# A decoder block on one core: longer runs for the table loads of the second half, fewer split buffers, four banks for the quad sums

## The chip, the core and the metric

The kernel runs on one core of a Trainium2 chip. The core has five engines that work through their own instruction streams and meet only at semaphores: TensorE (PE, matrix products, which loads its weights beside them), VectorE (DVE), ScalarE (ACT), GpSimd (POOL) and SyncE (SP, which here only issues DMAs). All DMAs of the core run on the same 16 DMA engines, whichever engine issued them. The metric is the time of one execution on the device in microseconds; the figure for a kernel is the median of several runs.

## The reference

One layer of a decoder for 256 tokens of width 2048, in float32, with two sub-layers and a last RMSNorm. The first mixes tokens (a recurrent branch and a state-space branch behind one projection). The second is the one that this change touches, a retrieval over 128 x 128 = 16384 single-neuron experts:

```python
h2 = rms_norm(x, norm2_g) * (1.0 + scale2) + shift2
# 8 heads; each picks its 16 best experts out of 16384 by product keys; gate = softmax of the 16 scores
u = jnp.take(u_tab, e, axis=0)                       # the chosen rows of the table u, 2048 wide
act = jax.nn.gelu(jnp.einsum("td,thkd->thk", xt, u))
v = jnp.take(v_tab, e, axis=0)                       # the same rows of the table v
out = jnp.einsum("thk,thkd->td", g * act, v)
return x + gate2 * out                               # then the last RMSNorm
```

So each token needs 128 rows of the table u for dot products, and 128 rows of the table v for a weighted sum.

## The kernel before

The experts are ordered in 128 columns of 128. Their first 100 columns are handled in a mixed way, the last 28 densely.

**The u quads** (`u_quad`, from line 1488). For the first 100 columns all dot products are computed: 25 quads of four columns, each 256 tokens x 512 experts. A quad takes eight items of the table u; an item is 128 x 1024 floats, 512 KB. An item holds, for the four columns of its quad, 256 of the 2048 features (two blocks of 128). A float32 product is made of three products of parts that TensorE takes at full speed, so a product of a and b is high(a) x high(b), low(a) x high(b), high(a) x low(b): lines 1496 to 1498, twelve matmuls for each item, each 512 wide. The sums of a quad lie in two of the banks 0, 1, 2, taken in turn, one for each half of the tokens. ACT copies them out (line 1502) to the tile X2, and a store writes them to memory.

**The stream of items** (lines 130 to 160). All weights and tables go through one list of items in the order of use. `issue_dma` loads the next item into one of four buffers `raw` (NRAW). `issue_split` makes an item's high part on ACT (line 149, L149), and one item later `issue_lo` makes its low part on DVE (line 158, L158), into one of four tiles `hl` (NHL), and then issues the load of the item that takes the buffer. `take` gives the next `hl` to the matmuls. A tile `hl` is free for a split when TensorE has finished the item four places before. Loads of u items of the quads are issued by SP; from the u slots on, SP and ACT issue them in turn.

**The sparse quads.** Of the first 100 columns each token uses only some 100 experts. When the lists of the chosen experts are ready, POOL gathers the dot products by address (words, line 1572, into `lsm`), ACT and DVE make the weights from them (`w_make`, the tiles Wz), and POOL gathers the rows of v, 128 rows of 8 KB at a time, into one of seven row buffers (tk, vx, vq; line 1559). `v_quad` (line 1607) multiplies four gathers with their weights: 16 matmuls, which the trace shows as 32, into the banks 4 to 7. There are 54 such quads in three groups: 12 for the first half of the tokens from the first 44 columns, then 27 for the second half of the tokens, then 15 for the first half again. `tick`, called once for each item of a u quad and of a slot, decides while the program is written where the next sparse quad stands in TensorE's order (`due`), and feeds POOL's queue (`w_feed`, `v_feed`). Nothing is decided on the chip.

**The dense rest.** 28 u slots (`u_slot`, two items each) and 56 v slots (`v_slot`, one item each, line 1714) handle the last 28 columns without gathers: 4 KB runs, half a row of the table for each partition.

**The end of a group.** The sums of the first group are copied by ACT to the tile S0 (line 1613). Those of the second group are scaled by gate2 and added to x on DVE directly from the banks (`merge`, lines 1741 and 1743, four times). `rows_load` loads the rows of x and of gate2 into the four parts of the tile R["t"] (named H in the trace): gate2 into part 3 at v slot 0, x of the second half into part 1 at slot 2, x of the first half into part 0 at slot 6; at slot 14 DVE scales S0 and adds it to part 0 in two instructions of 128x2048. The second group's last sparse quad is held until eight ticks behind the load of part 1 (the condition with `sq["rows"]` in `tick`).

Of the kernel before, what the change touches and what calls it, by code (L numbers as in the profile page):

```python
# [8 lines left out]
FT = mybir.dt.float32  # L9
FR = mybir.dt.float32r  # L10
# [19 lines left out]
GL = GA + GB  # L30
NQD = 2 * GL
NF = 4
NRAW = 4
NHL = 4
GD = 3
ADA_SSD, ADA_LRU, ADA_OUT = 0.65, 1.1, 0.74

N0 = 12
# [25 lines left out]
def hybrid_kernel(ctx, tc, xT, cols, w_ada, w_in, lru_w, w_o1, w_o2, w_q, keys, u_t, v_t, fng, out):  # L64
# [55 lines left out]
    for e in range(NQ, 16):  # L120
        for h in range(2):
            items.append(w_q[e][:, h * 1024:(h + 1) * 1024])

    for n in range(J1 // 4):
        for kp in range(8):
            items.append(u_t[4 * n:4 * n + 4, :, kp * 256:(kp + 1) * 256].rearrange("j p c -> p j c"))
    n_alt = len(items)
    items.extend(u_t[J1 + jj][:, h * 1024:(h + 1) * 1024] for jj in range(JD) for h in range(2))
    items.extend(v_t[J1 + jj][:, h * 1024:(h + 1) * 1024] for h in range(2) for jj in range(JD))

    st = {"dma": 0, "split": 0, "use": 0, "lag": 2}
    raws, hls, los = {}, {}, []

    def issue_dma():
        n = st["dma"]
        if n < len(items):
            raws[n] = wp.tile([128, 1024], FT, name="raw", bufs=NRAW)
            o = raws[n]
            if len(items[n].shape) == 3:
                o = o.rearrange("p (e c) -> p e c", e=items[n].shape[1])  # L140
            (act if n >= n_alt and n % 2 else sp).dma_start(o, items[n])
            st["dma"] += 1

    def issue_split():
        n = st["split"]
        if n < len(items):
            r = raws.pop(n)
            t = wp.tile([128, 2, 1024], FR, name="hl", bufs=NHL)
            act.activation(t[:, 0], r, AF.Copy)  # L149
            hls[n] = t  # L150
            st["split"] += 1
            los.append((t, r))
        issue_lo(st["lag"] if n < len(items) else 0)

    def issue_lo(keep):
        while len(los) > keep:
            t, r = los.pop(0)
            dve.tensor_sub(t[:, 1], r, t[:, 0].bitcast(FT))  # L158
            issue_dma()

    def take():
# [180 lines left out]
    for n in range(8):  # L342
        ada_group(n)
        if n == 2:
            for _ in range(NRAW):
                issue_dma()
        mid()
    issue_split()
    while any(stages):
# [1135 lines left out]
    ads2 = [dram.tile([T, x], FT, name=f"ad{i}") for i, x in enumerate((EA, EB))]  # L1485
    g2d = dram.tile([1, D], FT, name="g2d")

    def u_quad(n, pay):
# [110 lines left out]
    def v_quad(q):  # L1599
        tb, m = quads[q]  # L1600
        a, b = (0, GA) if tb == 0 and m < GA else (GA, GL) if tb == 0 else (0, GL)
        if m == a:
            for c in range(4):
                sb[c] = bank(4 + c)
        for c in range(4):
            for g in range(4):
                pe.matmul(sb[c][32 * g:32 * g + 32, :], Wz[:, q % NW, g], buf[4 * q + g][:, c * 512:(c + 1) * 512],  # L1607
                          start=(m == a), stop=(m == b - 1), skip_group_check=True)
# [40 lines left out]
    def tick():  # L1649
        if not sq["on"]:  # L1650
            return
        sq["it"] += 1
        sq["tk"] = n = sq.get("tk", 0) + 1
        if n == sq.get("seam"):
            sq["stored"][1] = True
        w_feed(4 if n > 8 else 1)
        w_make()
        v_feed()
        q, a = sq["n"], sq["a"] + 12
        due = 1 + (2 * GA - 1) * (n - 6) // (a - 6) if n <= a else 2 * GA + (NQD - 2 - 2 * GA) * (n - a) // (sq["all"] - a)  # L1660
        if (q < due and n >= sq["last"] + 2 and sq["made"] > q and sq["g"] >= 4 * q + 4
                and sq["it"] >= max(rt[q] + 3, mt[q] + 2) and not (q == GA + GL - 1 and sq.get("rows", n) > n - 8)):
            sq["last"] = n
            sparse()

# [58 lines left out]

    def rows_load(n):
        if n == 0:
            sp.dma_start(R["t"][:, 3], bass.AP(tensor=g2d.tensor, offset=g2d.offset, ap=[[0, 128], [1, D]]))
        elif n == 1:
            sp.dma_start(R["t"][:, 1], x2d[128:256, :])
            sq["rows"] = sq["tk"]  # L1730
        elif n == 4:
            sp.dma_start(R["t"][:, 0], x2d[:128, :])
        elif n == 2:
            dve.tensor_tensor(S0, S0, R["t"][:, 3], op=OP.mult)
            dve.tensor_tensor(R["t"][:, 0], R["t"][:, 0], S0, op=OP.add)
        else:
            sp.dma_start(R["t"][:, 2], bass.AP(tensor=fng.tensor, offset=fng.offset, ap=[[0, 128], [1, D]]))

    def merge(tb, c, ps):
# [1 line left out]
        dve.tensor_tensor(ps, ps, R["t"][:, 3, s], op=OP.mult)  # L1741
        a = R["t"][:, tb, s]
        dve.tensor_tensor(a, a, ps, op=OP.add)
        R[tb, c] = R.get((tb, c), 0) + 1
# [89 lines left out]
    for h in range(2):  # L1834
        for jj in range(JD):
            v_slot(h, jj)
            if h == 0 and jj in (0, 2, 6, 14):
                rows_load((0, 1, 4, 2)[(0, 2, 6, 14).index(jj)])
            elif h == 1 and jj == 0:
                rows_load(3)  # L1840
            tick()
    while sq["n"] < NQD - 1:
        tick()
# [79 lines left out]
```

## Time and profile before

| | before |
|---|---|
| median of 3 runs | 2027.33 us (2025.85 to 2032.89) |
| the profiled execution | 2030.7 us, its span 2027.4 us |
| busy PE, DVE, ACT, POOL | 96%, 67%, 44%, 35% of the span |
| mean granted clock of TensorE | 0.983 |
| mean DMA rate | 317 GB/s |
| stages, from the start of the span | projections and mixer to 843 us; u quads to 1546; u slots to 1766; v slots to 2004 |

The span runs from the first to the last instruction. A wait is put down to the instruction that ended it. Matmuls are pipelined, so PE's busy share says little by itself; idle time of PE and the granted clock say more. A DMA's time is that of its packets on the 16 engines. Rows of the profile give the line of the kernel (L149), the engine, the operation, the tile written and the tiles read, with shapes.

### The profile page before, as it was taken

What the parts mean: (1) busy time and instruction counts of PE and PEld (TensorE: products, weight loads), DVE (VectorE), ACT (ScalarE), POOL (GpSimd) and SP (SyncE); (2) the same over time, 40 slices, a digit from 0 to 9 for tenths busy, and PEclk for the clock granted to TensorE, in tenths of its full rate; (3) what the DMA queues carried; (4) which work ended last, traced back from release to release, by engine and by line L of the source; (5) the groups of instructions that cost most, each with busy time, mean ns of one, the idle gap of its engine ahead of it and who ended that gap; (6) DMA issues with size and microseconds to landing.
All of it is one profiled execution on the core that took longest, in us unless ns stands there. A gap on an engine that the chain in (4) does not pass through costs nothing.

```text
span 2027.4 us, 32778 instructions
## 1 busy us (share of the span) xinstructions
PE 1944.5 (96%) x12104; PEld 1534.1 (76%) x12104; DVE 1358.3 (67%) x2379; ACT 896.2 (44%) x1360; POOL 708.4 (35%) x599
## 2 busy tenths in 40 slices
PE   7999999999999999999999999999989999899997
PEld 4789999988999899888777666676657766665664
DVE  3368888899887887999997676742334443454444
ACT  3446666677653455444433333442333333332332
POOL 0003344242210110000112745464434766546563
PEclk9999999999999999999999999999989999999999
DMA  9967677768789865698876999999999999989996
GB/s 386 406 250 250 220 234 233 252 226 277 253 280 370 314 245 188 224 300 294 277 233 230 321 359 364 360 353 378 375 343 374 370 420 420 420 342 416 414 421 279
DMA packets 254531, 642.08 MB, mean 317 GB/s; under 512 B 25536, under 2 KB 130160, under 8 KB 227184
## 3 DMA queue, kind: packets, MB, share of 16 engines
q1 hardware_dynamic: 199184, 377.80, 53.6%
q0 software_dynamic: 38016, 215.49, 26.4%
q10 hardware_dynamic: 17168, 46.67, 6.2%
q8 instruction: 96, 1.57, 0.3%
q14 instruction: 67, 0.55, 0.1%
HBM read 633.67 MB, written 17.34 MB: 321 GB/s over the span
## 4 chain that ended last, share of the span: by engine, by line
PE 58%; DMA 23%; DVE 9%; issue 4%; ACT 3%; POOL 1%; SPq 0%; POOLq 0%; DVEq 0%; ACTq 0%
PE b L454 7%; DMA raw<-in_u_t 7%; PE b L1496 6%; PE b L1498 5%; PE b L1497 5%; DMA tk<-in_v_t,X 5%; PE b L1607 5%; DMA vq<-in_v_t,X 5%; PE b L456 4%; PE b L1714 3%; PE b L931 3%; DVE hl L158 3%; DMA lsm<-ad,X 3%; PE b L809 3%; PE b L810 2%
## 5 line engine op out<-in xcount | busy, mean ns | idle before, releaser
L149 ACT ACTIVATE hl<-raw 128x1024 fp32r<-128x1024 f32 x554 | 585.4, 1059 | 974.5 <-PE b L1498 230.0
L158 DVE TENSOR_TENSOR hl<-raw,hl 128x1024 fp32r<-128x1024 f32 x554 | 696.4, 1261 | 327.6 <-ACT hl L149 326.7
L454 PE MATMUL b<-H,hl 128*128 128x512 f32 x1056 | 376.6, 401 | 1.0 <-ACT X L675 1.0
L1496 PE MATMUL b<-hl,H 128*128 128x512 f32 x800 | 324.3, 405 | 13.0 <-ACT X L1502 8.2
L1498 PE MATMUL b<-hl,H 128*128 128x512 f32 x800 | 316.5, 396 | 2.8 <-DVE hl L158 2.5
L1497 PE MATMUL b<-hl,H 128*128 128x512 f32 x800 | 315.5, 394 | 0.0
L456 PE MATMUL b<-H,hl 128*128 128x256 f32 x1056 | 295.3, 280 | 2.4 <-DVE hl L158 2.4
L1572 POOL DMA_INDIRECT lsm<-ad,X x216 | 254.9, 1180 | 95.2 <-issue 63.4
L454 PEld LDWEIGHTS b<-H,hl 128*128 128x128 f32 x1056 | 198.4, 188 | 60.7 <-issue 11.0
L1559 POOL DMA_INDIRECT tk<-in_v_t,X x116 | 132.1, 1139 | 249.2 <-PE b L1607 168.2
L1607 PE MATMUL b<-tk,Wz 128*32 128x512 f32 x928 | 203.4, 598 | 6.7 <-DMA tk<-in_v_t,X 4.5
L456 PEld LDWEIGHTS b<-H,hl 128*128 128x128 f32 x1056 | 199.2, 189 | 4.0 <-DVE hl L158 3.1
L1496 PEld LDWEIGHTS b<-hl,H 128*128 128x128 f32 x800 | 152.6, 191 | 61.0 <-issue 15.1
L1607 PE MATMUL b<-vq,Wz 128*32 128x512 f32 x568 | 188.0, 602 | 3.6 <-DMA vq<-in_v_t,X 3.6
L1498 PEld LDWEIGHTS b<-hl,H 128*128 128x128 f32 x800 | 152.4, 191 | 39.5 <-DVE hl L158 6.6
L1497 PEld LDWEIGHTS b<-hl,H 128*128 128x128 f32 x800 | 152.8, 191 | 29.4
L1714 PE MATMUL b<-hl,X 128*128 128x512 f32 x672 | 162.2, 400 | 9.5 <-DVEq L1832 4.9
L1714 PEld LDWEIGHTS b<-hl,X 128*128 128x128 f32 x672 | 127.4, 192 | 50.8 <-issue 13.4
L809 PE MATMUL b<-H,hl 128*128 128x256 f32 x560 | 162.9, 291 | 0.4 <-DVE ggt L466 0.4
L811 PE MATMUL b<-H,hl 128*128 128x256 f32 x560 | 159.5, 285 | 1.3 <-DVE hl L158 1.3
L810 PE MATMUL b<-H,hl 128*128 128x256 f32 x560 | 159.5, 285 | 0.0
L394 DVE SCALAR_TENSOR_TENSOR adacc<-adr,cact,adacc 128x1024 f32<-128x1024 f32 x90 | 124.2, 1380 | 24.2 <-DMA adr<-in_w_ada 24.1
(388 smaller groups left out, 3137.7 us busy)
## 6 DMA issues: line engine op xcount, KB each, us to landing
raw<-in_u_t SPq DMA_DIRECT2D x228, 512.0 KB, 6.9
raw<-in_w_in SPq DMA_DIRECT2D x146, 512.0 KB, 4.9
adr<-in_w_ada SPq DMA_DIRECT2D x96, 512.0 KB, 5.1
adw<-in_w_ada SPq DMA_DIRECT2D x64, 512.0 KB, 10.2
raw<-in_w_o SPq DMA_DIRECT2D x64, 512.0 KB, 5.8
raw<-in_w_q SPq DMA_DIRECT2D x32, 512.0 KB, 4.3
raw<-in_u_t ACTq DMA_DIRECT2D x28, 512.0 KB, 8.4
raw<-in_v_t SPq DMA_DIRECT2D x28, 512.0 KB, 7.9
```

Source lines behind the costliest of these rows:

```text
L149: act.activation(t[:, 0], r, AF.Copy)
L158: dve.tensor_sub(t[:, 1], r, t[:, 0].bitcast(FT))
L454: pe.matmul(ps, w[:, 0, c], x[:, k].rearrange("p a b -> p (a b)"), start=(k == first), stop=False, skip_group_check=True)
L456: pe.matmul(ps[:, :256], w[:, 1, c], x[:, k, 0], start=False, stop=(k == 15), skip_group_check=True)
L809: pe.matmul(ps, wh, hT[:, k, 0, :], start=(k == 0), stop=False)
L810: pe.matmul(ps, wh, hT[:, k, 1, :], start=False, stop=False)
L1496: pe.matmul(o, hh, w[:, 0, :, kk], start=(k == 0), stop=False)
L1497: pe.matmul(o, hl_, w[:, 0, :, kk], start=False, stop=False)
L1498: pe.matmul(o, hh, w[:, 1, :, kk], start=False, stop=(k == 15))
L1572: pool.indirect_dma_start(wA[:, n % 32:n % 32 + 1], None, adf[i], bass.IndirectOffsetOnAxis(ap=LW[:, tb, g, m:m + 1], axis=0), bounds_chec ...
L1607: pe.matmul(sb[c][32 * g:32 * g + 32, :], Wz[:, q % NW, g], buf[4 * q + g][:, c * 512:(c + 1) * 512], start=(m == a), stop=(m == b - 1), s ...
L1714: pe.matmul(ob[tb * 2 + c], w[:, i, s], v[:, k, c * 512:(c + 1) * 512], start=(jj == 0 and (i, k) == (0, 0)), stop=(jj == JD - 1 and k == 1))
```

## The change

**The loads.** From the 83rd u item on (`n_r`; `n_x` and `n_r` are rounded from SX = 80) an item is no longer four columns x 256 features but two columns x 512 features: runs of 2 KB instead of 1 KB, the same 512 KB. Two such items hold what two items held before, so they make a pair: a split reads the half that it needs out of both. The four buffers `raw` become halves of two tiles `two8`. Past `n_x` the fourth tile `hl` becomes a third tile of loads: six buffers in three pairs, and three tiles `hl`. A split past that point may stand only when TensorE has taken the item three places before (`issue_split`), and a pair of buffers is loaded again when both its items have their low parts (`raw_free`).

The rows below are what SP issues at the end of the gate's loads and in the u quads (`raw<-in_u_t`: a load of a u item; S, vx: loads for gate2). Before:

```order
L1344 DMA vx<-in_w_ada 128x512
L141 DMA raw<-in_u_t 128x4x256 x2
L1344 DMA S_8026<-in_w_ada 128x512
L141 DMA raw<-in_u_t 128x4x256 x2
L1344 DMA S_8026<-in_w_ada 128x512
L141 DMA raw<-in_u_t 128x4x256 x124
L141 DMA raw<-in_u_t 128x1024 x4
```

and now:

```order
L1372 DMA vx<-in_w_ada 128x512
L164 DMA raw<-in_u_t 128x4x256 x2
L1372 DMA S_7802<-in_w_ada 128x512
L164 DMA raw<-in_u_t 128x4x256 x2
L1372 DMA S_7802<-in_w_ada 128x512
L164 DMA raw<-in_u_t 128x4x256 x6
L164 DMA raw<-in_u_t 128x2x512 x118
L164 DMA raw<-in_u_t 128x1024 x4
```

118 of the loads change their shape; their number and place stay.

**The banks.** Once the background work on TensorE is done (the lists of the experts and the weights for the u slots; the flag is `rows7`), bank 3 is free, and from the 21st quad on the quad sums alternate between two pairs of banks. The rows are ACT's around the end of one of the last quads, with the numbers of the banks (b0 to b3) and of the buffers (hl, raw: loads and parts; X2: the copied sums; lsm: gelus of words). Before:

```order
L149 ACTIVATE hl_14110<-raw_14060 128x1024
L1502 ACTIVATE X2_14127<-b0_13950 128x512
L1502 ACTIVATE X2_14127<-b1_13951 128x512
L149 ACTIVATE hl_14130<-raw_14079 128x1024
L1506 DMA ad1_8731<-X2_14127 128x2x512
L149 ACTIVATE hl_14190<-raw_14096 128x1024
...
L1502 ACTIVATE X2_14357<-b2_14176 128x512
L1502 ACTIVATE X2_14357<-b0_14177 128x512
```

and now:

```order
L176 ACTIVATE hl_13688<-raw_10467 128x1024
L1535 ACTIVATE X2_13703<-b0_13534 128x512
L1535 ACTIVATE X2_13703<-b1_13535 128x512
L176 ACTIVATE hl_13706<-raw_83 128x1024
L1539 DMA ad1_8484<-X2_13703 128x2x512
L176 ACTIVATE hl_13766<-raw_83 128x1024
...
L1535 ACTIVATE X2_13925<-b2_13752 128x512
L1535 ACTIVATE X2_13925<-b3_13753 128x512
```

The next quad took bank b0 again; now it takes two others, and buffers come in pairs of the same name.

**The v slots.** The second group's sums are copied by ACT to part 1 of R["t"], as the first group's are to S0, and the sums of both groups are scaled and added to x late, in four pieces of 512 columns at the v slots 17 to 20. The rows of x and gate2 are loaded at the slots 4, 8 and 12, the last norm's weights at slot 24. The condition that held the second group's last quad goes; in TensorE's order it stands one v slot earlier, behind the ninth in place of the tenth. The rows are SP's from the branch ahead of the v slots on (`H<-x2d`, `H<-g2d`, `H<-in_fng`: the rows of x, gate2 and the last norm). Before:

```order
L1727 DMA H<-g2d 128x2048
L141 DMA raw<-in_v_t 128x1024
L1729 DMA H<-x2d 128x2048
L141 DMA raw<-in_v_t 128x1024 x2
L1732 DMA H<-x2d 128x2048
L141 DMA raw<-in_v_t 128x1024 x11
L1737 DMA H<-in_fng 128x2048
```

and now:

```order
L164 DMA raw<-in_v_t 128x1024 x3
L1760 DMA H<-x2d 128x2048
L164 DMA raw<-in_v_t 128x1024 x2
L1762 DMA H<-g2d 128x2048
L164 DMA raw<-in_v_t 128x1024 x2
L1764 DMA H<-x2d 128x2048
L164 DMA raw<-in_v_t 128x1024 x6
L1771 DMA H<-in_fng 128x2048
```

The first three row loads stood behind none, one and three of SP's v loads and stand behind three, five and seven, in another order of x and gate2; the last one stood behind fourteen and stands behind thirteen.

**The feeding.** In `tick` the rows are fed before the words, and for eight ticks past the seam two words in place of four. POOL's queue holds the same rows in the same order before and after.

```diff
-NRAW = 4
-NHL = 4
+SX = 80
+RL = (4, 8, 12, 17, 18, 19, 20, 24)
...
+    n_x = (len(items) + SX) // 4 * 4
+    n_r = n_x + 4
     for n in range(J1 // 4):
         for kp in range(8):
-            items.append(u_t[4 * n:4 * n + 4, :, kp * 256:(kp + 1) * 256].rearrange("j p c -> p j c"))
+            if len(items) < n_r:
+                items.append(u_t[4 * n:4 * n + 4, :, kp * 256:(kp + 1) * 256].rearrange("j p c -> p j c"))
+            else:
+                j, c = 4 * n + 2 * (kp % 2), kp // 2 * 512
+                items.append(u_t[j:j + 2, :, c:c + 512].rearrange("j p c -> p j c"))
...
+    two8 = [wp.tile([128, 2, 1024], FT, name="raw", tag=f"raw{i}") for i in range(2)]
+    def raw_slot(n):
+        if n < n_r:
+            return two8[n % 4 // 2], n % 2
+        q, h = divmod(n - n_r, 2)
+        if q == 2 and len(two8) < 3:
+            two8.append(wp.tile([128, 2, 1024], FT, name="raw", tag="hl3"))
+        return two8[q % 3], h
+    def raw_free(n):
+        if n < n_r + 4:
+            return n - 4 < st["lo"]
+        if n < n_r + 6:
+            return n_x <= st["use"]
+        return ((n - 6) | 1 if n - 6 < n_alt else n - 6) < st["lo"]
...
     def issue_split():
         n = st["split"]
-        if n < len(items):
-            r = raws.pop(n)
-            t = wp.tile([128, 2, 1024], FR, name="hl", bufs=NHL)
-            act.activation(t[:, 0], r, AF.Copy)
+        if n < len(items) and (n < n_x + 3 or n - 3 < st["use"]):
+            t = wp.tile([128, 2, 1024], FR, name="hl", tag=f"hl{n % 4 if n < n_x else (n - n_x) % 3}")
+            a, h = raw_slot(n)
+            o, r = (t[:, 0], t[:, 1]), a[:, h]
+            if n_r <= n < n_alt:
+                r = a.rearrange("p a (j c) -> p (a j) c", j=2)[:, :, n % 2 * 256:(n % 2 + 1) * 256]
+                o = [x.rearrange("p (j c) -> p j c", j=4) for x in o]
+            act.activation(o[0], r, AF.Copy)
...
     def u_quad(n, pay):
-        ps = [bank((2 * n + tb) % 3) for tb in range(2)]
+        if qb[0] is None and sq["rows7"]:
+            x = (2 * n) % 3
+            qb[0] = [(x, 3), ((x + 1) % 3, (x + 2) % 3)]
+        ps = [bank(x) for x in (qb[0][n % 2] if qb[0] else ((2 * n) % 3, (2 * n + 1) % 3))]
...
-            if b == GA:
+            if b == GA or tb == 1:
                 for c in range(4):
-                    act.activation(S0[:, c * 512:(c + 1) * 512], sb[c], AF.Copy)
+                    act.activation((R["t"][:, 1] if tb else S0)[:, c * 512:(c + 1) * 512], sb[c], AF.Copy)
...
-        w_feed(4 if n > 8 else 1)
+        v_feed()
+        w_feed((4 if n < sq.get("seam", 999) or n > sq["seam"] + 8 else 2) if n > 8 else 1)
         w_make()
-        v_feed()
...
     def rows_load(n):
         if n == 0:
+            sp.dma_start(R["t"][:, 2], x2d[128:256, :])
+        elif n == 1:
             sp.dma_start(R["t"][:, 3], bass.AP(tensor=g2d.tensor, offset=g2d.offset, ap=[[0, 128], [1, D]]))
-        elif n == 1:
-            sp.dma_start(R["t"][:, 1], x2d[128:256, :])
-            sq["rows"] = sq["tk"]
-        elif n == 4:
+        elif n == 2:
             sp.dma_start(R["t"][:, 0], x2d[:128, :])
-        elif n == 2:
-            dve.tensor_tensor(S0, S0, R["t"][:, 3], op=OP.mult)
-            dve.tensor_tensor(R["t"][:, 0], R["t"][:, 0], S0, op=OP.add)
+        elif n < 7:
+            s = slice((n - 3) * 512, (n - 2) * 512)
+            for y, x, g in ((1, R["t"][:, 1], 2), (0, S0, 0)):
+                dve.tensor_tensor(x[:, s], x[:, s], R["t"][:, 3, s], op=OP.mult)
+                dve.tensor_tensor(R["t"][:, y, s], R["t"][:, g, s], x[:, s], op=OP.add)
```

More of the change, by code (lines that the diff above doesn't have):

```diff
@@ L122, in hybrid_kernel @@
             items.append(w_q[e][:, h * 1024:(h + 1) * 1024])
+    n_x = (len(items) + SX) // 4 * 4
+    n_r = n_x + 4
+    assert len(items) % 2 == 0
     for n in range(J1 // 4):
         for kp in range(8):
-            items.append(u_t[4 * n:4 * n + 4, :, kp * 256:(kp + 1) * 256].rearrange("j p c -> p j c"))
+            if len(items) < n_r:
[3 more added lines that the diff above has]
+                items.append(u_t[j:j + 2, :, c:c + 512].rearrange("j p c -> p j c"))
     n_alt = len(items)
@@ L129, in hybrid_kernel @@
     items.extend(v_t[J1 + jj][:, h * 1024:(h + 1) * 1024] for h in range(2) for jj in range(JD))
-    st = {"dma": 0, "split": 0, "use": 0, "lag": 2}
-    raws, hls, los = {}, {}, []
+    st = {"dma": 0, "split": 0, "use": 0, "lo": 0, "lag": 2}
+    two8 = [wp.tile([128, 2, 1024], FT, name="raw", tag=f"raw{i}") for i in range(2)]
+    hls, los = {}, []
+    def raw_slot(n):
[11 more added lines that the diff above has]
+        return ((n - 6) | 1 if n - 6 < n_alt else n - 6) < st["lo"]
     def issue_dma():
-        n = st["dma"]
-        if n < len(items):
-            raws[n] = wp.tile([128, 1024], FT, name="raw", bufs=NRAW)
-            o = raws[n]
+        while st["dma"] < len(items) and raw_free(st["dma"]):
+            n = st["dma"]
+            t, h = raw_slot(n)
+            o = t[:, h]
             if len(items[n].shape) == 3:
@@ L145, in issue_split @@
         n = st["split"]
-        if n < len(items):
-            r = raws.pop(n)
-            t = wp.tile([128, 2, 1024], FR, name="hl", bufs=NHL)
-            act.activation(t[:, 0], r, AF.Copy)
+        if n < len(items) and (n < n_x + 3 or n - 3 < st["use"]):
[6 more added lines that the diff above has]
+            act.activation(o[0], r, AF.Copy)
             hls[n] = t
             st["split"] += 1
-            los.append((t, r))
+            los.append((o, r))
         issue_lo(st["lag"] if n < len(items) else 0)
@@ L156, in issue_lo @@
         while len(los) > keep:
-            t, r = los.pop(0)
-            dve.tensor_sub(t[:, 1], r, t[:, 0].bitcast(FT))
+            o, r = los.pop(0)
+            dve.tensor_sub(o[1], r, o[0].bitcast(FT))
+            st["lo"] += 1
+        if st["dma"]:
             issue_dma()
@@ L344, in hybrid_kernel @@
         if n == 2:
-            for _ in range(NRAW):
-                issue_dma()
+            issue_dma()
         mid()
@@ L1486, in hybrid_kernel @@
     g2d = dram.tile([1, D], FT, name="g2d")
+    qb = [None]
     def u_quad(n, pay):
-        ps = [bank((2 * n + tb) % 3) for tb in range(2)]
+        if qb[0] is None and sq["rows7"]:
+            x = (2 * n) % 3
+            qb[0] = [(x, 3), ((x + 1) % 3, (x + 2) % 3)]
+        ps = [bank(x) for x in (qb[0][n % 2] if qb[0] else ((2 * n) % 3, (2 * n + 1) % 3))]
         for kp in range(8):
@@ L1661, in tick @@
         if (q < due and n >= sq["last"] + 2 and sq["made"] > q and sq["g"] >= 4 * q + 4
-                and sq["it"] >= max(rt[q] + 3, mt[q] + 2) and not (q == GA + GL - 1 and sq.get("rows", n) > n - 8)):
+                and sq["it"] >= max(rt[q] + 3, mt[q] + 2)):
             sq["last"] = n
@@ L1743, in merge @@
         dve.tensor_tensor(a, a, ps, op=OP.add)
-        R[tb, c] = R.get((tb, c), 0) + 1
+        R[tb, c] = R.get((tb, c), tb) + 1
         if R[tb, c] == 2:
@@ L1836, in hybrid_kernel @@
             v_slot(h, jj)
[L1837 to L1840, printed above, removed]
+            if h == 0 and jj in RL:
+                rows_load(RL.index(jj))
             tick()
```

## The prediction

> **What bounds the kernel now.** I read the windows first, cut where the program changes its stage: busy time of TensorE (PE), PE's weight loads, VectorE (DVE), ScalarE (ACT), GpSimd (POOL), then the granted PE clock, the DMA share and GB/s.
>
> ```profile
> 1078.00:1305.00 227.00, 216.56 (x1344) 152.21 (x1343) 156.13 (x387) 84.21 (x138) 113.12 (x92) 0.98 0.92 332
> 1305.00:1378.00 73.00, 72.37 (x426) 49.84 (x425) 35.01 (x66) 26.98 (x43) 44.99 (x36) 1.00 0.99 368
> 1378.00:1500.00 122.00, 108.39 (x540) 73.89 (x542) 42.61 (x51) 38.15 (x46) 49.75 (x45) 0.93 0.98 366
> 1500.00:1546.00 46.00, 46.00 (x238) 32.96 (x231) 17.04 (x21) 15.77 (x19) 21.06 (x18) 1.00 0.99 375
> 1546.00:1766.00 220.00, 217.85 (x1376) 152.02 (x1375) 93.44 (x152) 76.74 (x126) 141.50 (x121) 1.00 0.99 400
> 1766.00:1817.00 51.00, 46.05 (x241) 30.62 (x240) 26.90 (x46) 17.67 (x29) 23.91 (x23) 0.93 0.89 342
> 1817.00:2004.00 187.00, 176.48 (x948) 112.51 (x947) 83.35 (x135) 59.80 (x102) 114.52 (x99) 0.98 1.01 415
> ```
>
> By the count of L149's splits the first stretch begins at u item 78 and ends near 138; the next three hold the rest of the 200 items of the u quads; then come the u slots and the v slots. PE is full nearly everywhere, and so is the DMA. Only from 1378 to 1500 does PE lose much within the quads: 108.39 of 122 us busy, at 0.93 of the clock. Next the waits of that stretch, PE's and then ACT's longest:
>
> ```profile
> PE b L1496 <- ACT X L1502: 8.2, 2, 7.9
> PE b L1496 <- ACT hl L149: 4.8, 2, 4.3
> PE b L1498 <- DVE hl L158: 0.5, 1, 0.5
> ```
>
> ```profile
> ACT hl L149 <- DMA raw<-in_u_t: 62.3, 21, 9.0
> ```
>
> PE waits 13.5 us, and the clock costs 122 x 0.07 = 8.5 us more: 22.0 us. Behind all of it stand loads: ACT spends 62.3 of 122 us waiting for them. The longest stop in order of time (start, length, engine, line):
>
> ```profile
> 1477.91 0.39 PE L1496 MATMUL b<-hl,H 128*128 128x512 f32 x1
> ...
> 1480.63 0.39 PE L1496 MATMUL b<-hl,H 128*128 128x512 f32 x1
> ...
> 1481.77 0.39 PE L1498 MATMUL b<-hl,H 128*128 128x512 f32 x1
> 1483.93 1.06 ACT L149 ACTIVATE hl<-raw 128x1024 fp32r<-128x1024 f32 x1 [7.12 <-DMA raw<-in_u_t]
> ...
> 1485.02 1.23 DVE L158 TENSOR_TENSOR hl<-raw,hl 128x1024 fp32r<-128x1024 f32 x1 [6.75 <-ACT hl L149]
> ...
> 1488.46 1.06 ACT L149 ACTIVATE hl<-raw 128x1024 fp32r<-128x1024 f32 x1 [3.38 <-DMA raw<-in_u_t]
> 1489.42 1.06 ACT L1502 ACTIVATE X<-b 128x512 f32<-128x512 f32 x2
> ...
> 1490.05 0.80 PE L1496 MATMUL b<-hl,H 128*128 128x512 f32 x1 [7.90 <-ACT X L1502]
> ```
>
> ACT works in order: the copies that free the last quad's banks (L1502) stand behind two splits (L149) that wait for loads. The first two rows are 12 matmuls apart, one item: 2.72 us.
>
> **Why the loads are late.** The DMA view of a stretch inside such a wait, q0 being the gathers and q1 the loads; then of one with loads alone in 1 KB runs (1471 to 1475), and of one early on with loads alone in 2 KB runs (50 to 120):
>
> ```profile
> DMA packets 758, 2.91 MB, mean 416 GB/s; under 512 B 80, under 2 KB 450, under 8 KB 450
> q0 software_dynamic: 371, 2.52, 85.8%
> q1 hardware_dynamic: 386, 0.38, 15.3%
> ```
>
> ```profile
> DMA packets 1540, 1.55 MB, mean 387 GB/s; under 512 B 55, under 2 KB 1536, under 8 KB 1536
> ```
>
> ```profile
> DMA packets 14696, 28.43 MB, mean 406 GB/s; under 512 B 862, under 2 KB 862, under 8 KB 14688
> q1 hardware_dynamic: 14688, 28.32, 104.7%
> ```
>
> In 7.0 us (1463 to 1470) 371 packets of gathers and 386 of loads went: one for one, though a row of a gather is 8 KB and a run of a load 1 KB. So loads get 15% while gathers are queued. The Trainium skill (DMA: Bandwidth & Descriptors, "Queues, rings and completion order") has each engine drain a whole packet, typically 9 to 17 descriptors, from one ring before it turns to the next. If that held here as a fixed amount of bytes, the share would not move with the run; the counts above speak for one run a turn.
>
> **The change, part by part.** Everything up to item 78 (about 1078 us) stands in the same order with the same waits.
>
> *2 KB runs, 118 loads, six buffers.* The chain shows the beat of the quads when nothing is late:
>
> ```profile
> 1497.22 3.57 PE b L1607 x32
> 1514.62 3.57 PE b L1607 x32
> 1532.01 3.57 PE b L1607 x32
> ```
>
> 17.4 us for one sparse quad (3.57) and five items (13.6). It needs four gathers of 128 rows x 8 KB, 4.19 MB, five loads of 0.524 MB, and 5/8 of a 0.524 MB store, some 0.8 us. Now: the gathers take 4.19/2.52 x 7.0 = 11.6 us and 0.63 MB of loads pass with them, 1.2 items. The 17.4 - 11.6 - 0.8 = 5.0 us left give 1.93 MB at 387 GB/s, 3.7 items. That is 4.9 for 5 used. After: a 1 KB packet took 0.153 x 7.0 x 16/386 = 44 ns, a 2 KB one 1.047 x 70 x 16/14688 = 80 ns. The 386 turns last 386 x 36 ns/16 = 0.9 us more, the burst 13.1 us, and 1.26 MB pass, 2.4 items; 3.5 us at 406 GB/s give 2.7 more: 5.1 for 5. A burst now draws the store of items down by 11.6/3.48 - 1.2 = 2.1, then by 13.1/3.48 - 2.4 = 1.4; two that touch by 4.2 of the 8 items that four buffers and four pairs of parts hold, then by 2.8 of 9. So the lateness should mostly go. The margin of 0.1 item is thin: I keep one stop of half the size, 4 us. Bounds: 0 to all of 22.0. Term: -18.
>
> *Three pairs of parts and the pairing.* A split now follows the end of the third item before, not the fourth. Split and low part are these rows of the page:
>
> ```profile
> L149 ACT ACTIVATE hl<-raw 128x1024 fp32r<-128x1024 f32 x554 | 585.4, 1059 | 974.5 <-PE b L1498 230.0
> L158 DVE TENSOR_TENSOR hl<-raw,hl 128x1024 fp32r<-128x1024 f32 x554 | 696.4, 1261 | 327.6 <-ACT hl L149 326.7
> ```
>
> 2.3 us in the 5.44 us of the two items between: hidden, with 3.1 us to spare (before 5.8). ACT and DVE were 16 to 38% and 35 to 69% busy in the windows from 1078 on, so queues there are short. Splits that read four pieces of 256 aren't in the trace; I take the same row for them, and up to 3.1 us more would still be hidden. Term: 0. A pair waits for its second load: 1.3 us with the DMA free, up to 13.1/2.4 = 5.5 us inside a burst; rival B.
>
> *Four banks.* From the 21st quad on two pairs alternate. L1502 has then a whole quad, 8 x 2.72 = 21.8 us, before PE needs its bank. Its 8.2 us are inside the 22.0, and the low part of 1485.02 + 1.23 would have held PE to 1486.2 anyway: of 7.9 us the banks alone are worth 3.8.
>
> *Feeding order.* GpSimd's 1254 rows are the same before and after, so rows before words, and two words for four, change no queue: 0.
>
> *The v slots.* The waits from 1766 to 2006, and DVE's groups there:
>
> ```profile
> PE b L1714 <- DVEq L1832: 4.9, 1, 4.9
> PE b L1714 <- DVE H L1743: 4.5, 2, 4.0
> PE b L1607 <- DMA tk<-in_v_t,X: 3.5, 2, 1.9
> PE b L1607 <- DMA vq<-in_v_t,X: 2.5, 2, 1.9
> ```
>
> ```profile
> L1741 DVE TENSOR_TENSOR b<-b,H 128x512 f32<-128x512 f32 x9 | 6.3, 695 | 13.4 <-PE b L1714 12.5 <-PE b L1607 0.9
> L1743 DVE TENSOR_TENSOR H<-H,b 128x512 f32<-128x512 f32 x9 | 6.2, 688 | 0.3
> L1735 DVE TENSOR_TENSOR H<-H,S 128x2048 f32<-128x2048 f32 x1 | 2.3, 2293 | 0.0
> ```
>
> The first two waits stay: the branch and the merges at the half. One sparse quad moves a slot earlier, so its four row buffers come free 2.7 us sooner; gathers are what PE waits for after it (6.0 us in all), so up to -2.5. Against it, two row loads leave the loose stretch (342 GB/s) for the full one (415): 1.05 MB is 2.5 us each, up to +5; by their slots (8 and 12 of 56) I count one. On DVE 8 merges (5.5 us) and two wide sums (4.6) go, and 16 sums of 128x512 come, at 0.69 us 11.0; 2.8 us a slot for four slots of about 4.1 us, of which DVE has half free. The excess, some 0.7 us x 4, lies under the two items split ahead. ACT gets four copies, 4 x 0.6 us by L1502's row. Net 0, bounds -3 to +5.
>
> **The sum.** -18 + 0 + 0 + 0 = -18 us. The profiled execution spans 2027.4 us (2030.7 us as timed); the span becomes 2009, and from the median of 2027.3 the forecast is 2009 us.
>
> **Rivals.** A: the DMA is full by bytes (0.98 to 0.99 in the windows), so that turns only decide who waits, and the gain is the shorter packets: 118 x 0.524 MB x (1/387 - 1/406) = 7.5 us, 2020 us. For it: 4.9 and 5.1 are both near 5. Against: the quads average 366 GB/s where 416 were moved in a burst, so room is left. Chance 0.20.
>
> B, slower: the pair starves. ACT's split waits for two loads, and everything behind it on ACT, the banks' copies and the gelus of the words, waits too. A pair is issued when the low part of the pair three before it is done, seven items ahead: 7 x 3.48 - 2 x 2.3 = 19.8 us. In a burst 2.4 items take 13.1 us; with another pair queued ahead two pairs need 21.8 us, more than 19.8, so it decides wherever two bursts touch. At 11 us a stop (half of 22.0), six such in 14 beats would be 66 - 22 = +44: 2071 us; three, +11: 2038. I take 2050. Against it: the waits above hold only two stops over 4 us. Chance 0.07.
>
> C: the quads gain, the v slots give back: the sums of the second group leave their banks by ACT, behind splits that wait, and PE stands for one more wait of 4.3 us with 3.4 us of half clock behind it: 2009 + 8 = 2017 us. Chance 0.10.
>
> D: a turn is an amount of bytes, so the run leaves the share at 15%; as in A only 7.5 us come: 2020 us. Chance 0.04. It is what the rule of the Trainium skill (DMA: Bandwidth & Descriptors, "Queues, rings and completion order") comes to if its packets are filled by bytes.
>
> **The numbers.** Forecast 0.59, A 0.20, C 0.10, B 0.07, D 0.04. A difference under 0.3%, 6 us, can't be told from none. The forecast's own range is 2003 to 2018. Faster: 0.59 + 0.10 and about half of A and D (their 7.5 us lies just past 6), 0.80; slower 0.07; the same 0.13. The range goes down to 27 us gained (22.0, the quad's 2.5, and 2 or 3 for a deeper store), and up to nearly no gain: 2000 to 2026.
>
> **What would show it.** In the quads' second half: no PE wait for L1502 and next to none for hl; clock 1.00; beats of 17.4 us throughout; in a burst one load packet per gather packet, now of 2 KB, at 23 to 26% of the engines. Wrong if PE's waits there stay above 10 us (A, D), if ACT's waits for raw grow past 62 us (B), or if the v slots, 238 us from 1766 to 2004, last over 243 us (C).

## The result, and the profile after

| | before | changed |
|---|---|---|
| median of 6 runs each | 2026.59 us (2020.21 to 2032.89) | 2013.39 us (2009.36 to 2019.56) |
| ratio | | 0.9935, 95% interval 0.9907 to 0.9963 |
| the profiled execution's span | 2027.4 us | 2008.2 us |

The change saves 13.2 us, and by the interval between 7.5 and 18.9. The forecast was 2009 us, range 2000 to 2026. The two profiled executions lie further apart (19.2 us) than the medians: the one of before is above its median, the one of the changed kernel below.

The windows of the changed kernel, with the columns as in the prediction (PE, its weight loads, DVE, ACT, POOL, then clock, DMA share, GB/s):

```profile
1305.00:1378.00 73.00, 72.88 (x423) 50.64 (x421) 32.37 (x55) 27.82 (x43) 44.96 (x36) 1.00 0.96 366
1378.00:1500.00 122.00, 117.55 (x615) 79.96 (x614) 44.95 (x53) 41.09 (x49) 57.61 (x51) 0.99 1.01 400
1500.00:1546.00 46.00, 45.31 (x251) 33.38 (x250) 18.12 (x23) 17.44 (x24) 20.16 (x18) 1.00 0.99 393
```

In the stretch 1378 to 1500 PE is busy for 117.55 us, for 108.39 before, at a clock of 0.99 for 0.93, and the DMA moves 400 GB/s for 366. The waits of PE and then of ACT in it:

```profile
PE b L1529 <- ACT hl L176: 3.4, 2, 3.1
PE b L1531 <- DVE hl L185: 1.1, 2, 0.5
```

```profile
ACT hl L176 <- PE b L1531: 55.7, 23, 5.5
ACT hl L176 <- DMA raw<-in_u_t: 23.1, 5, 7.8
```

PE waits 4.5 us for 13.5, and no longer for the copies of the banks. ACT waited 62.3 us for loads there and now waits 23.1, and mostly for PE, which means that the parts lie ready before they are needed. The DMA inside a burst of gathers (q0) with loads (q1) queued, 1370 to 1384:

```profile
DMA packets 1473, 5.88 MB, mean 420 GB/s; under 512 B 239, under 2 KB 239, under 8 KB 929
q0 software_dynamic: 737, 4.45, 76.0%
q1 hardware_dynamic: 735, 1.41, 26.1%
```

Packets still go one for one, 737 and 735, now with 2 KB in each of the loads': 26.1% of the engines for 15.3%. Most signs that the prediction had named for its mechanism are there: no wait for L1535's copies in this stretch, the share of the loads, the clock at 0.99. The beat of 17.4 us throughout is not: the sparse quads that start at 1379.7 and 1404.2 stand 24.6 us apart. The experiments show that the mechanism was not the cause.

### The profile page after: what moved, and what is told of

The parts are those of the page before. It is cut to its first block, busy times and chain, and to the rows that moved or that the text cites. A ratio compares the mean times of both kernels' runs of the same rounds, so it can differ in the third digit from the quotient of the medians.

```text
span 2008.2 us, 32773 instructions
## 1 busy us (share of the span) xinstructions
PE 1937.0 (96%) x12104; PEld 1525.2 (76%) x12104; DVE 1357.7 (68%) x2385; ACT 899.8 (45%) x1364; POOL 713.5 (36%) x599
## 5 line engine op out<-in xcount | busy, mean ns | idle before, releaser
L1530 PE MATMUL b<-hl,H 128*128 128x512 f32 x800 | 312.9, 391 | 0.0
L1529 PEld LDWEIGHTS b<-hl,H 128*128 128x128 f32 x800 | 150.9, 189 | 52.9 <-issue 15.1
L1531 PEld LDWEIGHTS b<-hl,H 128*128 128x128 f32 x800 | 150.9, 189 | 39.8 <-DVE hl L185 7.4
L1530 PEld LDWEIGHTS b<-hl,H 128*128 128x128 f32 x800 | 151.2, 189 | 29.1
```

The costliest lines, as they stand in the source:

```text
L1529: pe.matmul(o, hh, w[:, 0, :, kk], start=(k == 0), stop=False)
L1530: pe.matmul(o, hl_, w[:, 0, :, kk], start=False, stop=False)
L1531: pe.matmul(o, hh, w[:, 1, :, kk], start=False, stop=(k == 15))
```

## The experiments

Twelve kernels ran in three groups of four, each group on one chip together with the kernel before; ratios are to the kernel before of the same group. A short table first. "Quads" is the time from the first sparse quad's first matmul to the last high x high matmul of a u quad, read from the start times in the trace of one execution: the stretch in which loads and gathers meet. In the third group the kernel before took 2045.66 us, for 2029.32 and 2026.31 in the others, so its quads are compared only among themselves. A single execution says little below 10 us: before, v slots alone, and v slots alone with the rows early run the same instructions in this stretch, and their quads take 410.5, 402.2 and 412.6 us.

| kernel | group | us | ratio (95%) | quads |
|---|---|---|---|---|
| before (profile shown) | | | | 410.5 |
| changed (profile shown) | | | | 396.7 |
| loads alone | 1 | 2011.45 | 0.9915 (0.9883 to 0.9946) | 392.4 |
| banks alone | 1 | 2026.16 | 0.9981 (0.9959 to 1.0004) | 407.9 |
| v slots alone | 1 | 2035.06 | 1.0031 (1.0014 to 1.0048) | 402.2 |
| changed, in 1 KB runs | 1 | 2015.14 | 0.9934 (0.9907 to 0.9961) | 394.0 |
| six buffers alone | 2 | 2006.57 | 0.9901 (0.9881 to 0.9921) | 390.4 |
| 2 KB runs in four buffers | 2 | 2081.69 | 1.0252 (1.0225 to 1.0279) | 456.3 |
| changed without v slots' edits | 2 | 2012.97 | 0.9934 (0.9913 to 0.9956) | 393.2 |
| changed, again | 2 | 2013.61 | 0.9935 (0.9913 to 0.9957) | 394.1 |
| five buffers alone | 3 | 2032.95 | 0.9920 (0.9888 to 0.9952) | 401.6 |
| pairs' rule in four buffers | 3 | 2035.98 | 0.9944 (0.9914 to 0.9974) | 412.0 |
| six buffers and banks | 3 | 2029.36 | 0.9908 (0.9877 to 0.9939) | 402.1 |
| v slots alone, rows early | 3 | 2039.50 | 0.9980 (0.9951 to 1.0008) | 412.6 |

### The parts alone

**Loads alone**: the kernel before, with the items, `raw_slot`, `raw_free`, `issue_dma` and `issue_split` of the change, and nothing else of it. The order on PE and POOL is that of before.

> The kernel before with the loads of the change alone: 118 loads in 2 KB runs in pairs, six buffers, three pairs of parts; banks and v slots as before. Theory R (run length: one packet a turn, so a load of 2 KB runs gets 22% of a burst for 15%): it carries nearly all of the change, ratio 0.993 to 0.995 (-10 to -14 us), and PE's waits between 1378 and 1500 fall from 13.5 to under 6 us. Theory K (the banks carry it, because the copies behind a waiting split were the longest stop): at most 4 us of the gain is here, ratio 0.998 or more, and a stop of some 4 us or more on L1502's successor stays. Theory V (the v slots carry a part): -13 less what the v slots give.

Measured 0.9915, 17.9 us less and somewhat beyond theory R's range: the loads carry the gain. PE's waits from 1135 to 1525 in its profile:

```profile
PE b L1497 <- DVE LG L1488: 3.0, 1, 3.0
PE b L1524 <- ACT hl L176: 1.1, 1, 1.1
PE b L1497 <- DVE Wt L1507: 0.9, 3, 0.5
PE b L1526 <- DVE hl L185: 0.7, 2, 0.5
```

There is no wait on the copies (L1530 there) any more, though the banks are three as before: with loads in time the copies don't stand behind a waiting split. Theory K is out.

**Banks alone**:

```diff
-        ps = [bank((2 * n + tb) % 3) for tb in range(2)]
+        if qb[0] is None and sq["rows7"]:
+            x = (2 * n) % 3
+            qb[0] = [(x, 3), ((x + 1) % 3, (x + 2) % 3)]
+        ps = [bank(x) for x in (qb[0][n % 2] if qb[0] else ((2 * n) % 3, (2 * n + 1) % 3))]
```

> The kernel before with the four banks alone; all instructions in the same order, only the last five quads' sums lie in other banks. Theory R: the low parts come late all the same, so 3.8 us at most of the profile's 7.9 us stop, ratio 0.998 to 1.000. Theory K: 8.2 us of waits on L1502 and half of the 8.5 us of lost clock go, -8 to -12 us, ratio 0.994 to 0.996.

0.9981 is 3.9 us, as large as the 3.8 of theory R, though the interval reaches just past no change. The waits from 1135 to 1525 have what was argued from the low part:

```profile
PE b L1501 <- ACT hl L149: 5.2, 5, 3.1
PE b L1503 <- DVE hl L158: 2.4, 5, 0.6
PE b L1501 <- ACT X L1507: 0.7, 1, 0.7
```

The wait for the copies falls from 8.2 us to 0.7, but PE then waits for the late parts themselves.

**V slots alone**: the copies by ACT, the late scaling, the row loads at slots 4, 8, 12 and 24, and no condition on the second group's last quad.

> The kernel before with the edits of the v slots alone: second group's sums copied by ACT and scaled late, rows loaded at slots 4, 8, 12 and 24, the 39th sparse quad one v slot earlier. The prediction: net 0, between -3 and +5 us, ratio 0.9985 to 1.0025. Rival C (the v slots give back, PE stands once more with half clock behind it): +8 us, ratio 1.004, and a PE wait of 4 us on ACT's copies. A theory in which the row loads' move out of the full stretch counts: +5 us, 1.0025.

1.0031, 6.3 us slower: outside the bounds of -3 to +5 at the median, though the interval (2.8 to 9.7 us) overlaps them. Its profile shows none of the new wait of rival C: PE's waits in the v slots are of the kinds of before, for the branch, the merges at the half and the gathers. From the first v product to the last it takes 237.1 us, for 232.5 before. Another 4.5 us were lost ahead of the v slots, at the start of the u slots (PE's longest wait from 1500 to 1760):

```profile
PE b L455 <- ACT X L1503: 4.5, 1, 4.5
```

The other kernel with these edits alone (the rows early, below) has the same wait, 4.2 us, and no other profile has it. Up to there both run the instructions of before in the order of before, so whether the edits bring it about in some way, or chance, isn't shown.

### Run length or buffers

**The changed kernel in 1 KB runs**: the same pairs, buffers, parts, banks and v slots; the order on PE, POOL, DVE and ACT is the same word for word.

```diff
-            if len(items) < n_r:
+            if True:
...
-            if n_r <= n < n_alt:
+            if False:
```

> The changed kernel with its 118 loads in 1 KB runs of four columns again; six buffers in pairs, three pairs of parts, four banks and the v slots stay. Theory R: the share of loads in a burst falls back to 15%, a burst draws 2.1 items again from a store of 9 for 8, and most of the gain goes: ratio to the kernel before 0.997 to 1.000. Theory S (the store of six buffers carries it, the run length does not matter): as fast as the changed kernel, 0.993 to 0.994. Rival A (bytes bound, only the shorter packet time counts, 7.5 us): 0.9965 to 0.998.

0.9934, as the changed kernel. The run length, on which the largest term of the prediction was built, is worth nothing that can be seen here (the intervals leave some 0.3% either way). Theory R and rival A fall, and S is left. The second group takes the two apart without anything else.

**Six buffers alone**: the kernel before, 1 KB runs, six buffers, three tiles of parts, each buffer loaded again by itself.

```diff
-            raws[n] = wp.tile([128, 1024], FT, name="raw", bufs=NRAW)
+        if n < n_r + 6:
+            return n_x <= st["use"]
+        return n - 6 < st["lo"]
...
-            t = wp.tile([128, 2, 1024], FR, name="hl", bufs=NHL)
+            t = wp.tile([128, 2, 1024], FR, name="hl", tag=f"hl{n % 4 if n < n_x else (n - n_x) % 3}")
```

> The kernel before with six buffers and three tiles of parts alone: 1 KB runs of four columns as before, each buffer loaded again by itself, no pairs; banks and v slots as before. Theory S (loads are issued earlier, run length does not matter): as fast as the change's loads in full, ratio 0.990 to 0.994, ACT's waits for loads between 1135 and 1525 some 30 to 45 us for 86. Theory R (run length decides, and the changed kernel in 1 KB runs was fast for its four banks): 0.996 to 0.999, waits for loads over 60 us.

0.9901, 2006.57 us: more than the whole change. Its windows' row, PE's waits and ACT's waits from 1378 to 1500:

```profile
1378.00:1500.00 122.00, 120.99 (x639) 83.58 (x638) 45.79 (x55) 42.63 (x52) 67.14 (x54) 1.00 1.05 406
```

```profile
PE b L1526 <- DVE hl L185: 0.5, 1, 0.5
PE b L1524 <- ACT X L1530: 0.3, 1, 0.3
```

```profile
ACT hl L176 <- DMA raw<-in_u_t: 46.8, 13, 8.3
```

PE stands 0.8 us of 122, at full clock, and the DMA moves 406 GB/s. ACT still waits 46.8 us for loads, but PE does not notice. From 1135 to 1525 ACT's waits for loads are 59.3 us for 86.2 before: more than the 30 to 45 that theory S expected, and just under the 60 of theory R. The time, though, lies where theory S put it (0.990 to 0.994). A burst there (1397 to 1403) is as it was before, one for one and 15% for the loads:

```profile
q0 software_dynamic: 331, 2.19, 86.6%
q1 hardware_dynamic: 329, 0.33, 15.4%
```

So the share of a burst need not change. What changes is the stretch behind it. The kernel before right behind its stop, 1391 to 1400, with no gathers (the first row has the rate in 40 equal slices), and below it ACT in that stretch (start, length, work, idle time before it):

```profile
GB/s 382 378 378 373 369 364 387 382 341 300 164 105 82 73 36 50 168 264 232 228 291 355 382 282 146 87 68 150 164 187 159 178 218 182 246 177 287 296 328 355
DMA packets 2070, 2.16 MB, mean 240 GB/s; under 512 B 67, under 2 KB 1971, under 8 KB 2069
...
q1 hardware_dynamic: 1967, 1.95, 70.5%
```

```profile
1393.95 1.06 ACT L149 ACTIVATE hl<-raw 128x1024 fp32r<-128x1024 f32 x1 [0.40 <-DMA raw<-in_u_t]
1394.92 1.07 ACT L1502 ACTIVATE X<-b 128x512 f32<-128x512 f32 x2
1395.87 1.05 ACT L149 ACTIVATE hl<-raw 128x1024 fp32r<-128x1024 f32 x1
...
1400.67 1.06 ACT L149 ACTIVATE hl<-raw 128x1024 fp32r<-128x1024 f32 x1 [3.74 <-PE b L1498]
...
1406.21 1.06 ACT L149 ACTIVATE hl<-raw 128x1024 fp32r<-128x1024 f32 x1 [1.75 <-DMA raw<-in_u_t]
```

The rate falls twice. Near 1394.3 it is down to 36 GB/s: the items that landed are being split one behind the other, and a buffer is loaded again only behind its low part. At 1396.9 all parts are made and ACT waits 3.74 us for PE; no tile of parts is free, so the buffers stay full and loads have no room, 68 GB/s at the lowest. Over the 9 us it is 240 GB/s, with no gathers beside the loads. Less than 10 us later ACT waits for a load again. In the six-buffer kernel the loads run at full rate in such a pause, though a shorter one (1386 to 1391):

```profile
DMA packets 1947, 1.92 MB, mean 383 GB/s; under 512 B 104, under 2 KB 1943, under 8 KB 1943
q1 hardware_dynamic: 1891, 1.88, 106.3%
```

Two short stretches prove little, so the packets of the traces were counted from 1135 to 1523, in steps of half a microsecond. A step belongs to a pause where the gathers take less than 5% of the 16 engines' time; the second column has the time in pauses below 300 GB/s:

| kernel (one execution each) | pauses, us | of them below 300 GB/s, us |
|---|---|---|
| before | 110 | 36 |
| v slots alone (four buffers) | 100 | 32 |
| six buffers alone | 94 | 16 |
| changed | 86 | 25 |
| changed, in 1 KB runs | 94 | 14 |
| 2 KB runs in four buffers | 117 | 73 |
| pairs' rule in four buffers (group 3) | 118 | 42 |
| v slots alone, rows early (group 3, four buffers) | 112 | 42 |
| five buffers alone (group 3) | 101 | 22 |
| six buffers and banks (group 3) | 94 | 20 |

That six buffers with three tiles of parts are enough for the gain is shown by the run. That they act by filling the pauses is a reading of these rows and counts, which agree with it.

**2 KB runs in pairs, in the four buffers and four parts of before**:

```diff
-        q, h = divmod(n - n_r, 2)
-        if q == 2 and len(two8) < 3:
-            two8.append(wp.tile([128, 2, 1024], FT, name="raw", tag="hl3"))
-        return two8[q % 3], h
+        return two8[n % 4 // 2], n % 2
...
-        return ((n - 6) | 1 if n - 6 < n_alt else n - 6) < st["lo"]
+        return ((n - 4) | 1 if n - 4 < n_alt else n - 4) < st["lo"]
```

> The kernel before with the 2 KB runs in pairs alone, in its four buffers and four tiles of parts. Theory R (a longer run's share of a burst decides): most of the gain, ratio 0.991 to 0.995, ACT's waits for loads between 1135 and 1525 under 50 us. Theory S (the store decides): 0.997 or more; and since a pair in four buffers can be loaded again only when both its items have their low parts, a load is issued up to one item (2.7 us) later than before, so it may be slower, up to 1.005, with waits for loads of 86 us or more.

1.0252, 55 us slower, far beyond what either theory allowed. Windows, PE's longest waits and ACT's wait for loads from 1135 to 1525:

```profile
1135.00:1525.00 390.00, 342.69 (x1964) 229.55 (x1963) 187.46 (x398) 119.54 (x196) 182.97 (x153) 0.93 0.86 322
```

```profile
PE b L1490 <- DVE Wt L1500: 22.3, 8, 8.0
PE b L1490 <- DVE LG L1481: 13.4, 1, 13.4
PE b L1517 <- ACT X L1523: 5.1, 3, 3.2
```

```profile
ACT hl L169 <- DMA raw<-in_u_t: 157.7, 24, 14.6
```

The same stretch of the kernel before, ACT's row first:

```profile
ACT hl L149 <- DMA raw<-in_u_t: 86.2, 27, 9.0
```

```profile
PE b L1469 <- DVE LG L1460: 3.0, 1, 3.0
PE b L1469 <- DVE Wt L1479: 2.5, 4, 1.6
```

ACT waits 157.7 us for loads, for 86.2, up to 14.6 at a time, while the DMA's mean busy share is 0.86. PE's longest waits are not for the table's parts: they are for small work of DVE (L1500 and L1481, weights and lists), 35.7 us for 5.5 before, and that work stands behind the low parts in DVE's queue, which wait for the splits. One such stop, from the load that comes late on ACT to the product that PE holds back (timeline from 1318 to 1323.5, rows of other work left out):

```profile
1319.86 1.06 ACT L169 ACTIVATE hl<-raw 128x1024 fp32r<-128x1024 f32 x1 [7.44 <-DMA raw<-in_u_t]
...
1320.95 1.23 DVE L178 TENSOR_TENSOR hl<-raw,hl 128x1024 fp32r<-128x1024 f32 x1 [7.21 <-ACT hl L169]
...
1322.09 0.60 DVE L1500 SCALAR_TENSOR_TENSOR Wt<-b,Wt 128x112 f32<-128x112 f32 x2
...
1322.84 0.53 PE L1490 MATMUL b<-ohr,two 128*128 128x56 f16 x8 [5.76 <-DVE Wt L1500]
```

**The pairs' rule alone**: four buffers, 1 KB runs, each item split by itself, but a buffer loaded again only when its pair is done (the last two lines of the diff above, without the 2 KB items).

> The kernel before in four buffers and four tiles of parts with the pairs' rule alone: 1 KB runs, each item split by itself, but a buffer loaded again only when both items of its pair have their low parts. Theory P (the rule of pairs cost the 55 us of the 2 KB runs in four buffers: of four buffers one is idle for an item): ratio 1.015 to 1.03. Theory Q (the split that needs both loads of a pair cost it): 0.998 to 1.008.

0.9944: it costs nothing, so both theories missed. Its interval leaves out 1.000, yet nothing in the profile says why it should be faster: its quads take 412.0 us, as those of the kernel of that group with the v slots' edits (412.6), which has the loads of before. Both were profiled in executions some 11 us above their medians. So a difference of half a per cent in this group is not by itself a gain. The 55 us therefore need what this kernel lacks, the split that waits for both loads of a pair, or the 2 KB run itself; and with six buffers the same runs lose at most a few us. Pairs whose splits need both loads, in two pairs of buffers, are the reading left, by exclusion.

**Five buffers alone**: the six-buffer kernel with `% 5` for its buffers.

```diff
-        q, h = divmod(n - n_r, 2)
+        q, h = divmod((n - n_r) % 5, 2)
...
-        return n - 6 < st["lo"]
+        return n - 5 < st["lo"]
```

> The depth-only kernel (1 KB runs, each buffer by itself, three tiles of parts) with five buffers in place of six: buffers and parts are eight together, as before the change (4 and 4), only moved from parts to loads. Theory S-total (what counts is how many items buffers and parts hold together): as the kernel before, 0.998 to 1.002. Theory S-place (what counts is how many loads may be on their way, since buffers wait for gathers and parts do not): most of the 0.9901 of six buffers, 0.990 to 0.995, and ACT's waits for loads between 1135 and 1525 under 75 us for 86.

0.9920, as expected if the number of loads on their way counts. There is room for eight items as before, one of them moved from the parts to the loads. By the times alone it isn't settled: five buffers lie only 3.0 us below the pairs' rule in four buffers of the same group. The profiles point the same way as the ratio: the pauses hold 22 us below 300 GB/s, for 42 in the two kernels of the group with four buffers. So what counts is, as far as these runs show, how many loads may be on their way, not how much buffers and parts hold together; that would be why giving up a tile of parts was right. The third sign, ACT's waits for loads under 75 us from 1135 to 1525, can't be read: 26.7 us are named there, and 65.7 us are put down to nothing that the profile shows.

### What remains

**The changed kernel without the edits of the v slots, and the changed kernel beside it**:

> The changed kernel without the edits of the v slots: the change's loads and four banks. If the v slots give back what they cost in the kernel before (ratio 1.0031, some 6 us): 0.990, 2 to 9 us below the changed kernel run beside it. If they cost only where loads come late, or the ratio was an accident: as the changed kernel, 0.9935, within 2 us. Banks on top of these loads: under 1 us by all theories, since no PE wait on the copies was left with the loads alone.

> The changed kernel itself, beside the other three: ratio 0.9935 again, 0.991 to 0.996. All theories expect this; it is here so that the kernel without the v slots' edits has its partner on the same chip.

2012.97 and 2013.61: in the changed kernel the v slots' edits, and the feeding order, which the first of the two leaves out as well, are worth 0.6 us, which is nothing here. So the 6.3 us of these edits alone do not show in the change. In the two profiles the v slots take 235.9 us with the edits and 231.9 without, so a small cost there that the rest hides isn't ruled out.

**V slots alone, with the rows loaded at slots 0, 2 and 6**:

```diff
-RL = (4, 8, 12, 17, 18, 19, 20, 24)
+RL = (0, 2, 6, 17, 18, 19, 20, 24)
```

> The kernel before with the edits of the v slots alone, but the rows of x and gate2 loaded at v slots 0, 2 and 6 as before. If the ratio 1.0031 of those edits alone came of the row loads that stand in the full stretch: 1.000, within 0.002. If it came of the copies on ACT, the late scaling or the sparse quad one slot earlier: 1.003. If it was an accident of the runs: 1.000 too, and the waits of the v slots in the profile are as before.

0.9980, the interval takes in 1.000 and leaves out 1.0031. That may be the place of the row loads, or an accident of the first measurement. For the first speaks that the v slots take 232.5 us here, as before, for 237.1 with the rows late; against it, that three other kernels of this group take 237.1 to 239.9 us with the rows early. The runs can't tell the two apart, and since the changed kernel pays nothing clear of noise for the late rows, it stays open.

**Six buffers and banks**:

> The depth-only kernel (six buffers of 1 KB runs, three tiles of parts) with the four banks added, v slots as before. With no PE wait over 0.3 us on the copies left in the quads, the banks bring under 1 us: 0.990, 0.988 to 0.992, which is 5 to 8 us below the changed kernel (0.9935). If the banks are worth what they were alone (0.9981): 0.988.

0.9908, within its interval equal to six buffers alone in the second group (0.9901). The banks add nothing that can be seen once the loads are in time. Both ratios lie below the changed kernel's, the second by less than its interval. In the second group, side by side, six buffers alone took 2006.57 us and the changed kernel 2013.61: the simpler kernel is the best one measured. At one place the changed kernel is seen to lose. Its splits there stand in twos behind one long wait:

```profile
1380.47 2.00 ACT L176 ACTIVATE hl<-raw 128x1024 fp32r<-128x1024 f32 x2 [7.80 <-DMA raw<-in_u_t]
1382.38 1.07 ACT L1535 ACTIVATE X<-b 128x512 f32<-128x512 f32 x2
1388.14 1.06 ACT L176 ACTIVATE hl<-raw 128x1024 fp32r<-128x1024 f32 x1 [4.69 <-DMA raw<-in_u_t]
...
1397.78 2.01 ACT L176 ACTIVATE hl<-raw 128x1024 fp32r<-128x1024 f32 x2 [7.54 <-DMA raw<-in_u_t]
```

The sparse quads on either side stand 24.6 us apart there, 19.1 in the six-buffer kernel and 17.9 in the changed kernel in 1 KB runs, which splits each item by itself, read from their starts in the traces. So splits that need two loads do lengthen that beat. They don't explain the whole difference: the kernel in 1 KB runs has none of them, its next beat but one is 23.5 us for 20.1, and its ratio is the changed kernel's. The difference of 7 us between the changed kernel and the six-buffer kernel isn't placed.

## Why the prediction was right, and where it was wrong

**The quads, -18.** Sign, place and nearly the size hold; the mechanism does not. The step that failed is the supply per beat, "4.9 for 5 used" with 1 KB runs and "5.1 for 5" with 2 KB. The runs did raise the loads' share about as worked out (23 to 26%, measured 26.1), but 1 KB runs, with 15.4% in the six-buffer kernel, are as fast or faster. That the figure came near was luck as far as this step goes: the edit that paid was in the same change. The error sits in the sum of supply: it let the loads use all of the pause between bursts at 387 GB/s, and counted the store as the sum of buffers and parts. The trace of before could have told it: 240 GB/s in the pause at 1391, with ACT waiting for PE in it. The pause was short of buffers, not of bandwidth, so the small edit that the prediction took only as a store of nine items for eight was the one that paid.

**The size.** 13.2 us of the 18 came. The 22.0 us lost in 1378 to 1500 were those of one execution. The kernel with the v slots' edits alone has the same instructions in the same order up to the v slots, and lost in that stretch of its profile:

```profile
1378.00:1500.00 122.00, 114.98 (x585) 79.85 (x584) 44.09 (x54) 39.58 (x48) 61.40 (x51) 0.97 1.00 380
```

that is 7.0 us of idle PE and 122 x 0.03 = 3.7 of clock, 10.7 for 22.0. The step that failed is carrying a sum made on one execution to the median. What is left of the stops was sized well: 4 us, measured 4.5 us of waits and 1.2 of clock.

**Three pairs of parts, 0.** Right: with three the six-buffer kernel waits 0.5 us for a low part. **Pairing, 0, with rival B at 0.07.** In six buffers it costs, by the medians, no more than the 6 to 7 us between the changed kernel and the six-buffer kernel, which differ in the pairs, the runs, the banks, the feeding order and the v slots, none of the last three worth anything that can be seen there. In four buffers B's outcome is real, 55 us where B had put 23, and by a route like B's, with PE waiting for what is queued behind the late splits; B had named ACT's copies and gelus, and most of it was DVE's weights and lists. So the third pair of buffers is what the pairs need, again by exclusion.

**Four banks, inside the term, 3.8 alone.** Measured 3.9 alone, with an interval that reaches no change, and nothing that can be seen beside loads in time. **Feeding, 0.** Not separated by a run of its own, but the changed kernel without it and without the v slots' edits is as fast as the changed kernel.

**V slots, 0, with rival C at 0.10.** Right for the change as far as can be told: 0.6 us. PE's waits there from 1766 to 2006 are the same kinds as before:

```profile
PE b L1747 <- DVE H L1777: 4.8, 2, 4.0
PE b L1640 <- DMA vq<-in_v_t,X: 2.9, 1, 2.9
PE b L1640 <- DVE Wz L1620: 2.3, 1, 2.3
```

From the first v product to the last the changed kernel takes 234.0 us, before 232.5 (start times in the trace). Alone, the edits cost 6 us in one measurement, and nothing in another with the rows loaded early.

**Rivals A and D.** Both gave the 7.5 us of shorter packets. The changed kernel in 1 KB runs has the same ratio, so no such gain is seen, though 7.5 us is not far beyond what the intervals leave. D is out by the counts as well: 735 loads for 737 rows, with twice the bytes. The Trainium skill (DMA: Bandwidth & Descriptors, "Queues, rings and completion order") has an engine drain a packet of typically 9 to 17 descriptors before it turns to the next ring. The counts here agree with turns that take equally many runs from each queue, whatever their length. One run a turn gives such counts, and so do ten a turn: the counts can't tell them apart, and the prediction's "one run a turn" isn't shown.

## What to carry to other kernels

When loads come late behind bursts of another queue, look at the pauses between the bursts first: if the DMA runs below its rate there while the splitting engine waits for the matmuls, the loads may lack buffers, and in this kernel more loads on their way were worth more than a better share. Change the number of buffers alone before the shape of the loads; and don't let a step wait for two loads unless a third pair of buffers stands behind them. A sign that was predicted and is seen (the share) does not show its cause; only the run without it does.

## What the runs showed that was not expected

A late split costs most through what is queued behind it: of the 55 us of four paired buffers some 30 (35.7 less 5.5, in one execution of each kernel) are PE's waits for operands of small products that have nothing to do with the table.

The same program took 0.8 to 1% longer in the third group than in the others, 2045.66 us. ACT's waits from 1135 to 1525 have a far larger entry there that the profile can't name, here first of the five-buffer kernel in the third group, then of the six-buffer kernel in the second:

```profile
ACT hl L176 <- issue: 65.7, 20, 5.5
```

```profile
ACT hl L176 <- issue: 9.1, 2, 5.2
```

The entry is no longer idle time, only idle time without a name: in that stretch ACT is busy for 140.1 us in the first kernel and 145.0 in the second. So the named waits of the third group can't be set against those of the others. Whether the longer time is the chip, and what the entry stands for, is open.
